# Softmax weights of twelve heads turned by VectorE's blocks and a trip through DRAM instead of by TensorE

## The chip, the core and the metric

The kernel runs on one core of one Trainium2 chip. The core has five engines that run side by side, each through its own queue in order: TensorE (PE in the profile; PEld are its weight loads) multiplies matrices and turns tiles, VectorE (DVE) and ScalarE (ACT) work on elements, GpSimd (POOL) does small elementwise work and can issue transfers, SyncE (SP) issues transfers. Engines wait for one another by semaphores. The metric is the time of one execution in microseconds (us) on the device; the kernel before was run three times.

## The reference

Two layers of an encoder over 256 tokens with 2048 channels, float32. Each layer has a mixer with two kinds of attention, eight heads each, and a gated feed-forward part. Cut to the attention:

```python
def window_attention(q, k, v, sink):          # mixer A, 8 heads, 2 groups of k and v
    s = jnp.einsum('bnqgrd,bnkgd->bgrnqk', qb, kw) * (HEAD_DIM ** -0.5)
    s = jnp.where(mask, s, NEG_INF)
    m = jnp.maximum(jnp.max(s, axis=-1, keepdims=True), snk)
    p = jnp.exp(s - m)
    p = p / (jnp.sum(p, axis=-1, keepdims=True) + jnp.exp(snk - m))
    o = jnp.einsum('bgrnqk,bnkgd->bnqgrd', p, vw)

def neighbourhood_attention(q, k, v, bias_tab):   # mixer B, 8 heads
    s = jnp.einsum('brqhd,brikhd->bhrqik', qg, kg) * (HEAD_DIM ** -0.5)
    s = jnp.where(col_mask, s + bias, NEG_INF)
    p = jax.nn.softmax(s, axis=-1)
    o = jnp.einsum('bhrqik,brikhd->brqhd', p, vg)
```

The softmax weights p of a head are a 256 x 256 matrix. They are made with the query on the partitions, and the product with v needs them with the key on the partitions, so each head's p has to be turned.

## The kernel before, in words

All weights stream once from DRAM in units of 16 blocks of 128x128 (1 MB). `unit_steps` issues the load of a unit on SP's queue (line 286) into one of four buffers; ScalarE makes the high half of each half unit (the cast of line 297) and VectorE the low half (the subtraction of line 298), into one of four half-unit buffers `hl`; TensorE then makes three passes (high x high, high x low, low x high) per block, in `feature_block` (lines 314 to 316, results with features on the partitions) or in `Stream.tokens` (lines 377 to 379, results with tokens on the partitions). So a unit passes through SP, the DMA engines, ScalarE, VectorE and TensorE in this order, and on each engine the work of other units and of the attention stands between.

Work beside the stream is put in by `Paced`: at the end of each unit `tick` first runs what was deferred to it and then moves each background job on by its rate. One job is the list of adaLN columns (line 225 loads 1 MB on SP's queue into the same four buffers, line 226 multiplies and sums it on VectorE). The other is `attention`: one step of it moves each live head to its next `yield` and starts a new head if its q and k are there. In the second layer its rate is `ATT[1]`, 0.4 steps a unit, and from the projection of mixer A on `ATT_B[1]`, 0.21.

A head begins with the splits of its q and k (`in_halves`), then runs `attend`: the scores `sc` (line 607) on TensorE, mask or bias with the maximum on VectorE (line 610), the exponential and the scaling by 1/sum on ScalarE (lines 618 and 626), which leave p of 128 x 2 x 256 in SBUF. At the next step TensorE turns p in four pieces of 128x128 into PSUM (`tp`, line 631), ScalarE and VectorE split it into `pT` (lines 389 and 390, 128x512 each). At the step after that TensorE multiplies it with v (`po`, line 639) and the result is split into `oA` or `oB` (lines 641 and 642). Mixer B's heads load their bias into p first (line 825, on SP's queue). p has two buffers, pT one.

Between, groups of q and k are normalised by `qk_rows`: the sums of squares on ScalarE (line 547), the inverse root on GpSimd (line 441), which is nearly all that GpSimd does, and the multiplication on VectorE (line 556). Their turned rows lie in `packs`: `qTa` holds the eight q of mixer A, each 128x256; in mixer B's pack `b`, the rows `b[:, 8 + i]` hold q and `b[:, i]` hold k of head i. In the second layer q and k are copied into split halves (`SCORES_3`) before the scores, after which those rows are no longer read.

The order of instructions on each engine is set by the scheduler of the framework from the program's order and its own estimates; the order of the changed kernel's instructions is known from its build.

Of the kernel before, what the change touches and what calls it, by code (L numbers as in the profile page):

```python
# [9 lines left out]
F32 = mybir.dt.float32  # L10
F32R = mybir.dt.float32r
# [4 lines left out]
P = 128  # L16
L = 2
D = 2048
S = 256
# [8 lines left out]
NEG = -1e30  # L28
SCALE = HEAD ** -0.5
GRID_W, NA_KH, NA_KW = 64, 8, 16  # L30


QKV_GROUPS = [1024, 0, 512, 2560, 3584, 1536, 3072, 4096, 2048]
# [44 lines left out]

H_RATE = [2.7, 1.7]

ATT = [1.288, 0.4]
ATT_B = [0.21, 0.21]

SCORES_3 = (1,)

ADA_ORDER = [[p * KC + k for k in range(KC) for p in ps] for ps in ((0, 1), (2,), (3, 4), (5,))]
ADA_ORDER = [i for part in ADA_ORDER for i in part]
# [47 lines left out]
def encoder(ctx: ExitStack, tc: tile.TileContext, a: dict, out: bass.AP):  # L135
    nc = tc.nc
    pool = lambda name, bufs, **kw: ctx.enter_context(tc.tile_pool(name=name, bufs=bufs, **kw))
# [12 lines left out]
    ev = pool("ev", 3)  # L150
    at = pool("at", 2)
    sm = pool("sm", 3)
    mm = pool("mm", 4, space=bass.MemoryType.PSUM)
    ax = pool("ax", 3, space=bass.MemoryType.PSUM)

    ident = const.tile([P, P], F32, name="ident")
    make_identity(nc, ident[:])
# [25 lines left out]
    def place(tag, n, dt, name):  # L183
        return sp.tile([P, n, S], dt, name=name, tag=tag)
# [16 lines left out]
    def paired(dt, name):  # L201

        t = ev.tile([P, 2 * S + ROW], dt, name=name, tag="u", bufs=2)
        return t[:, ROW - OFF : ROW - OFF + 2 * S].rearrange("p (a s) -> p a s", a=2)
# [71 lines left out]
                pass  # L276

    bg = Paced()

    def unit_steps(l, u, by_halves=False):  # L280

        raw = rawp.tile([P, UB * P], F32, name=f"w{l}_{u}", tag="raw")
        if not by_halves:
            nc.sync.dma_start(raw[:], a["ws"][l, u])
        halves = []
        streamed = any(m == "w_in" and mo < GATE_A // P for m, _, mo in STREAMS[l][u * UB : (u + 1) * UB])
        at = OFF if streamed else 0
        for j in range(2):  # L290
            n = UB * P // 2
            hl = hlp.tile([P, 2 * n + ROW], F32R, name=f"hl{l}_{u}_{j}", tag="hl")
            hl = hl[:, at : at + 2 * n].rearrange("p (a n) -> p a n", a=2)
            r = raw[:, j * n : (j + 1) * n]
            if by_halves:
                nc.sync.dma_start(r, a["ws"][l, u][:, j * n : (j + 1) * n])
            nc.scalar.copy(hl[:, 0], r)  # L297
            nc.vector.tensor_tensor(out=hl[:, 1], in0=r, in1=hl[:, 0].bitcast(F32), op=ALU.subtract)  # L298
            halves.append(hl)
            if j == 0:  # L300
                yield halves
# [84 lines left out]
    def split(dst, src, scale=None):  # L386

        if scale is None:
            nc.scalar.copy(dst[:, 0], src)
            nc.vector.tensor_tensor(out=dst[:, 1], in0=src, in1=dst[:, 0].bitcast(F32), op=ALU.subtract)  # L390
            return
        nc.scalar.activation(out=dst[:, 0], in_=src, func=AF.Copy, scale=scale)
        nc.vector.scalar_tensor_tensor(
            out=dst[:, 1], in0=src, scalar=scale, in1=dst[:, 0].bitcast(F32), op0=ALU.mult, op1=ALU.subtract
        )
# [202 lines left out]
    def by(x):  # L598

        return ((0, 0), (0, 1), (1, 0))[: 2 * len(x) - 1]  # L600

    def attend(q, k, v, p, mask, scale, sink, o):

        sc = ax.tile([P, 2, S], F32, name="sc", tag="ax")
        for t in range(2):
            for i, j in by(q):
                nc.tensor.matmul(sc[:, t], q[i][:, t * P : (t + 1) * P], k[j], start=i + j == 0, stop=(i, j) == by(q)[-1])  # L607
        m = sm.tile([P, 2], F32, name="m", tag="m")
        for t in range(2):
            nc.vector.tensor_tensor_reduce(  # L610
                out=p[:, t], in0=sc[:, t], in1=mask[:, t], scale=scale, scalar=-3.0e38 if sink is None else sink,
                op0=ALU.add, op1=ALU.max, accum_out=m[:, t : t + 1],
            )
        nm = sm.tile([P, 2], F32, name="nm", tag="nm")
        nc.vector.tensor_scalar(out=nm[:], in0=m[:], scalar1=-1.0, scalar2=None, op0=ALU.mult)
        den = sm.tile([P, 2], F32, name="den", tag="den")
        for t in range(2):
            nc.scalar.activation(out=p[:, t], in_=p[:, t], func=AF.Exp, bias=nm[:, t : t + 1], accum_out=den[:, t : t + 1])
        if sink is not None:
            es = sm.tile([P, 2], F32, name="es", tag="es")  # L620
            nc.scalar.activation(out=es[:], in_=nm[:], func=AF.Exp, bias=sink)
            nc.vector.tensor_tensor(out=den[:], in0=den[:], in1=es[:], op=ALU.add)
        ri = sm.tile([P, 2], F32, name="ri", tag="ri")
        nc.vector.reciprocal(out=ri[:], in_=den[:])
        for t in range(2):
            nc.scalar.activation(out=p[:, t], in_=p[:, t], func=AF.Copy, scale=ri[:, t : t + 1])
        yield
        tp = ax.tile([P, 2, S], F32, name="tp", tag="ax")
        for k in range(2):
            for t in range(2):  # L630
                nc.tensor.transpose(tp[:, k, t * P : (t + 1) * P], p[:, t, k * P : (k + 1) * P], ident[:])  # L631
        pT = at.tile([P, 2, 2, S], F32R, name="pT", tag="pT", bufs=1)
        split(pT, tp[:])
        v = v()
        yield
        po = ax.tile([P, 512], F32, name="po", tag="ax")
        for i, j in by(v):
            for b in range(2):
                nc.tensor.matmul(po[:, :S], v[i][:, b], pT[:, j, b], start=i + j + b == 0, stop=i + b == 2)  # L639
        o = o()  # L640
        nc.scalar.copy(o[:, 0], po[:, :S])
        nc.vector.tensor_tensor(out=o[:, 1], in0=po[:, :S], in1=o[:, 0].bitcast(F32), op=ALU.subtract)
# [91 lines left out]
    tables = []  # L734
# [23 lines left out]
    for l in range(L):  # L758
# [35 lines left out]
        kTa, qTa = packs[0][:, 0:3:2], packs[0][:, 4:12]  # L794
# [3 lines left out]
        oA, oB = [], []  # L798

        def head_a(i):  # L800
            g = i // (HA // GA)
            if i >= 6:
                oA.append(paired(F32R, f"oA{l}_{i}"))
            elif i % 2 == 0:
                o = place(("y0", "y1", "y2")[i // 2], 4, F32R, f"oA{l}_{i}")
                oA.extend((o[:, :2], o[:, 2:]))
            q = in_halves(qTa[:, i], f"qA{l}_{i}", "qh", l in SCORES_3)
            if i % (HA // GA) == 0:
                kvs[0] = in_halves(kTa[:, g], f"kA{l}_{g}", "kh", l in SCORES_3)
            k = kvs[0]  # L810
            yield
            p = at.tile([P, 2, S], F32, name="p", tag="p")

            def v():
                if i % (HA // GA) == 0:
                    kvs[1] = in_halves(packs[0][:, 1:4:2, g * HEAD : (g + 1) * HEAD], f"vA{l}_{g}", "vh", True)
                return kvs[1]

            yield from attend(q, k, v, p, tables[0], SCALE, sink[:, i : i + 1], lambda: oA[i])

        def head_b(hb):
            b, i = packs[1 + hb // 4], hb % 4
            v = b[:, 4:8].rearrange("p (t a) s -> p t (a s)", t=2)
            p = at.tile([P, 2, S], F32, name="p", tag="p")
            nc.sync.dma_start(p[:], a["bias"][l, hb])
            q = in_halves(b[:, 8 + i], f"qB{l}_{hb}", "qh", l in SCORES_3)
            k = in_halves(b[:, i], f"kB{l}_{hb}", "kh", l in SCORES_3)
            yield
            yield from attend(
                q, k, lambda: in_halves(v[:, :, i * HEAD : (i + 1) * HEAD], f"vB{l}_{hb}", "vh", True), p, p, 1.0, None,  # L830
                lambda: oB_of(hb),
            )

        def oB_of(hb):
            if hb == 0:
                o = place("a", 12, F32R, f"oB{l}_{hb}")
                oB.extend(o[:, 2 * i : 2 * i + 2] for i in range(6))
            elif hb == 6:
                oB.extend(chunks_of(sp, "b0", 6, f"oB{l}_{hb}", 2))
            return oB[hb]  # L840
# [30 lines left out]
        for pi, (groups, gates) in enumerate(parts):  # L871
            last = pi == len(parts) - 1
            for g, part in enumerate(groups):
                have_h(part)
                pss = st.tokens(h, part)
                if pi == max(0, len(parts) - 2) and g == 0:
                    gains, sink, cw, rots = small(l)
                dst = packs[g // 3][:, 4 * (g % 3) : 4 * (g % 3) + 4]
                rows = dst.rearrange("p (t a) s -> p t (a s)", t=2)
# [25 lines left out]
                if g == 2:  # L905
                    bg.add(job, ATT[l])

# [26 lines left out]
        if l:  # L934
            bg.pace(job, ATT_B[l])
        gb = []
        for tag in ("y0", "y1", "y2"):
            t = place(tag, 4, F32, f"gb{l}_{tag}")
            gb += [t[:, i] for i in range(4)]
        for i in range(2):  # L940
            t = paired(F32, f"gb{l}_{i}")
# [56 lines left out]
        for gi, chunks in enumerate(FF_GROUPS):  # L998
# [34 lines left out]
            for cs in sets:  # L1033
                fns = [lambda p, e=e, c=c: e(p, c) for c in cs for e in (g_evac, v_evac)]
                src = bare.chunks if gi == 0 and cs[0] < BARE[1] // 2 else bare.h
# [113 lines left out]
```

## Time and profile before

| | us |
|---|---|
| median of 3 runs | 2667.84 |
| lowest and highest run | 2664.56, 2676.24 |
| span of the profiled execution | 2663.2 |
| first layer, first and last of TensorE's turns of p, from the span's start | 281.1, 443.7 |
| second layer, the same | 1518.7, 1796.0 |

The span is that of the profiled execution, from the first to the last instruction. The profile lists for each group of instructions its line, engine, operation, what it writes and reads, shapes, count, busy time and the mean length of one. A timeline gives the start and the length of single instructions and, in brackets, how long the engine was idle before and who released it. The chain of waits goes back from the last instruction to what released each step, so what stands on it sets the time. SPq are SP's issues of transfers.

### The profile page before, as it was taken

To read this page: it belongs to the slowest core of one execution; us is meant where nothing else is said; L and a number is where in the kernel's file an instruction comes from. 1 tells how busy PE (TensorE), PEld (TensorE's weight loads), DVE (VectorE), ACT (ScalarE), POOL (GpSimd) and SP (SyncE) were. 2 spreads that over 40 slices of the span, in tenths; PEclk is the share of its full clock that TensorE was granted. 3 is DMA by queue.
4 is the path that set the end of the run, shared out by engine and by line. 5 is a ranking of instruction groups with operands and counts; after the bars stand their busy time and mean duration, and the time that the engine had idled before them with its cause. 6 is when DMAs were issued, how large, how long until landed. Compare 5 with 4: busy or idle time off the path is not lost.

```text
span 2663.2 us, 50845 instructions
## 1 busy us (share of the span) xinstructions
PE 2650.9 (100%) x21256; PEld 2565.7 (96%) x21256; DVE 2102.2 (79%) x2959; ACT 1412.8 (53%) x2284; POOL 36.2 (1%) x25
## 2 busy tenths in 40 slices
PE   9999999999999999999999999999999999999999
PEld 7888899999999999999998889999999999999999
DVE  8898998997987888788976667768888866655664
ACT  5445865456644555355555566554565445544553
POOL 0001100000000000000000000000000000000000
PEclk9999999999999999999999999999999999999999
DMA  9987789885787878788766666666747765555554
GB/s 372 351 327 292 262 300 352 317 320 199 291 294 287 302 288 295 289 294 289 290 217 254 228 229 231 245 252 253 285 173 288 297 256 190 190 194 194 197 191 143
DMA packets 102039, 700.41 MB, mean 263 GB/s; under 512 B 12721, under 2 KB 15025, under 8 KB 17969
## 3 DMA queue, kind: packets, MB, share of 16 engines
q1 hardware_dynamic: 101810, 697.17, 71.4%
q8 instruction: 166, 2.72, 0.4%
q14 instruction: 63, 0.52, 0.1%
HBM read 695.03 MB, written 2.10 MB: 262 GB/s over the span
## 4 chain that ended last, share of the span: by engine, by line
PE 89%; DVE 6%; ACT 1%; issue 1%; DMA 1%; POOL 0%; SPq 0%; DVEq 0%; ACTq 0%
PE ps L314 25%; PE ps L316 25%; PE ps L315 25%; PE ps_t L377 4%; PE ps_t L379 4%; PE ps_t L378 4%; DVE hl L298 2%; DVE aw L226 2%; DMA aw<-in_aw 1%; PE sc L607 1%; PE po L639 1%; ACT hl L297 1%; PE tp L631 1%; POOL qrs L441 0%; PE qtp L580 0%
## 5 line engine op out<-in xcount | busy, mean ns | idle before, releaser
L298 DVE TENSOR_TENSOR hl<-w,hl 128x1024 fp32r<-128x1024 f32 x928 | 1128.3, 1222 | 360.0 <-ACT hl L297 357.6
L297 ACT CAST hl<-w 128x1024 fp32r<-128x1024 f32 x928 | 970.7, 1049 | 748.5 <-PE ps L316 518.1
L314 PE MATMUL ps<-h,hl 128*128 128x256 f32 x3328 | 922.8, 277 | 1.3 <-DVE ya L915 0.6
L315 PE MATMUL ps<-h,hl 128*128 128x256 f32 x3328 | 919.8, 276 | 0.0
L316 PE MATMUL ps<-h,hl 128*128 128x256 f32 x3328 | 919.8, 277 | 0.0
L314 PEld LDWEIGHTS ps<-h,hl 128*128 128x128 f32 x3328 | 624.8, 188 | 2.4 <-DVE ya L915 0.8
L315 PEld LDWEIGHTS ps<-h,hl 128*128 128x128 f32 x3328 | 625.3, 188 | 0.4 <-DVE h L470 0.2
L316 PEld LDWEIGHTS ps<-h,hl 128*128 128x128 f32 x3328 | 624.4, 188 | 0.0
L226 DVE CUSTOM_DVE_ANT_0 aw<-aw,cact,ab 128x2048 f32<-128x2048 f32 x189 | 443.5, 2347 | 48.8 <-DMA aw<-in_aw 47.8
L377 PE MATMUL ps_t<-hl,h 128*128 128x512 f32 x576 | 223.1, 392 | 2.6 <-ACT h L469 2.1
L378 PE MATMUL ps_t<-hl,h 128*128 128x512 f32 x576 | 224.9, 391 | 0.3
L379 PE MATMUL ps_t<-hl,h 128*128 128x512 f32 x576 | 224.3, 390 | 0.0
L994 DVE SCALAR_TENSOR_TENSOR u<-ps,cw,u 128x255 f32<-128x255 f32 x304 | 146.1, 481 | 66.5 <-ACT u L992 62.2
L992 ACT ACTIVATE u<-ps,cw 128x256 f32<-128x256 f32 x152 | 85.9, 565 | 187.9 <-PE ps L316 187.5
L316 PE MATMUL ps<-merged,hl 128*128 128x256 f32 x512 | 141.8, 277 | 0.4 <-DVE hl L298 0.4
L315 PE MATMUL ps<-merged,hl 128*128 128x256 f32 x512 | 141.6, 277 | 0.0
L314 PE MATMUL ps<-merged,hl 128*128 128x256 f32 x512 | 141.6, 277 | 0.0
L315 PE MATMUL ps<-act_o,hl 128*128 128x256 f32 x512 | 141.4, 276 | 0.0
L316 PE MATMUL ps<-act_o,hl 128*128 128x256 f32 x512 | 141.3, 276 | 0.0
L314 PE MATMUL ps<-act_o,hl 128*128 128x256 f32 x512 | 141.2, 276 | 0.0
L377 PEld LDWEIGHTS ps_t<-hl,h 128*128 128x128 f32 x576 | 107.9, 188 | 26.1 <-ACT h L469 3.1
L378 PEld LDWEIGHTS ps_t<-hl,h 128*128 128x128 f32 x576 | 108.1, 188 | 23.7 <-DVE hl L298 1.9
(231 smaller groups left out, 4612.5 us busy)
## 6 DMA issues: line engine op xcount, KB each, us to landing
w<-in_ws SPq DMA_DIRECT2D x463, 1024.0 KB, 4.9
aw<-in_aw SPq DMA_DIRECT2D x189, 1024.0 KB, 6.1
p<-in_bias SPq DMA_DIRECT2D x16, 256.0 KB, 4.2
x<-in_xT SPq DMA_DIRECT2D x4, 512.0 KB, 5.3
aw_o<-in_aw SPq DMA_DIRECT2D x2, 1024.0 KB, 12.3
out<-x SPq DMA_DIRECT2D x16, 128.0 KB, 2.1
w<-in_ws SPq DMA_DIRECT2D x2, 512.0 KB, 11.7
aw_b<-in_aw SPq DMA_DIRECT2D x1, 1024.0 KB, 18.1
```

The source lines that it names most:

```text
L226: nc.vector.tensor_tensor_reduce(out=raw[:], in0=raw[:], in1=cact[:], scale=1.0, scalar=ab[:, i : i + 1], op0=ALU.mult, op1=ALU.add, accum ...
L297: nc.scalar.copy(hl[:, 0], r)
L298: nc.vector.tensor_tensor(out=hl[:, 1], in0=r, in1=hl[:, 0].bitcast(F32), op=ALU.subtract)
L314: nc.tensor.matmul(out, hi, act[0], start=first, stop=False)
L315: nc.tensor.matmul(ps[:, :S], hi, act[1], start=False, stop=False)
L316: nc.tensor.matmul(out, lo, act[0], start=False, stop=last)
L377: nc.tensor.matmul(ps[:], xh, hi, start=kc == kcs[0], stop=False)
L378: nc.tensor.matmul(ps[:], xh, lo, start=False, stop=False)
L379: nc.tensor.matmul(ps[:], xl, hi, start=False, stop=kc == kcs[-1])
L607: nc.tensor.matmul(sc[:, t], q[i][:, t * P : (t + 1) * P], k[j], start=i + j == 0, stop=(i, j) == by(q)[-1])
L992: nc.scalar.activation(out=u, in_=ps, func=AF.Identity, scale=w[:, 1:2], bias=w[:, 3:4])
L994: nc.vector.scalar_tensor_tensor(out=u[:, to], in0=ps[:, of], scalar=w[:, j : j + 1], in1=u[:, to], op0=ALU.mult, op1=ALU.add)
```

## The change

Twelve heads of the second layer, the first six of each mixer (`MOVED`), no longer turn p on TensorE. `attend` takes `rows`, two stretches of 128x256 that nothing reads any more: for mixer A the head's own q in `qTa` and a spare tile (tag "r", two buffers), for mixer B the head's own q and k in `b`. VectorE's `transpose` turns p in blocks of 32x32 into these rows, one instruction for each half of the queries. GpSimd's queue then writes them to a DRAM tile `pY` (two buffers): for each half and each 32 partitions one transfer, eight in a head, each of 32 KB in 256 pieces of 128 bytes that bring every block to its place. Three units later (`BACK`, by way of `later`), or when the head needs it, SP's queue brings the two halves back into the same rows, 128 KB each; SP waits there for all eight writes. Two steps more than before lie between, then ScalarE and VectorE split the rows into `pT`, two pieces of 128x256 each. The rates become `ATT[1]` 0.42 and `ATT_B[1]` 0.32. The other four heads of the second layer and all of the first stay as they were.

```diff
+BLOCK = 32
...
-ATT = [1.288, 0.4]
-ATT_B = [0.21, 0.21]
+ATT = [1.288, 0.42]
+ATT_B = [0.21, 0.32]
...
+BACK = 3
+MOVED = [(0, 0), (6, 6)]
...
+    dram = pool("dram", 2, space=bass.MemoryType.DRAM)
...
+    def once(fn):
+        due = [fn]
+        def run():
+            if due:
+                due.pop()()
+        return run
+
+    def later(n, fn):
+        if n == 0:
+            fn()
+        else:
+            bg.defer(lambda: later(n - 1, fn))
+
+    def turned_blocks(p, rows):
+        y = dram.tile([P, 2, S], F32, name="pY", tag="pY")
+        to = y[:].rearrange("(b i) k (t a j) -> t a i k b j", i=BLOCK, t=2, a=P // BLOCK)
+        for t, row in enumerate(rows):
+            nc.vector.transpose(out=row, in_=p[:, t])
+            src = row.rearrange("p (k b j) -> p k b j", k=2, j=BLOCK)
+            for a in range(P // BLOCK):
+                nc.gpsimd.dma_start(to[t, a], src[a * BLOCK : (a + 1) * BLOCK])
+        return y
...
-    def attend(q, k, v, p, mask, scale, sink, o):
+    def attend(q, k, v, p, mask, scale, sink, o, rows=None):
...
+        if rows is not None:
+            rows = rows()
+            y = turned_blocks(p, rows)
+            def back():
+                for k in range(2):
+                    nc.sync.dma_start(rows[k], y[:, k])
+            back = once(back)
+            later(BACK, back)
+            yield
+            yield
+            back()
+            pT = at.tile([P, 2, 2, S], F32R, name="pT", tag="pT", bufs=1)
+            for k in range(2):
+                split(pT[:, :, k], rows[k])
+        else:
             tp = ax.tile([P, 2, S], F32, name="tp", tag="ax")
...
+            def rows():
+                spare = ev.tile([P, S], F32, name=f"spare{l}_{i}", tag="r", bufs=2)
+                return [qTa[:, i], spare[:]]
...
+                q, k, v, p, tables[0], SCALE, sink[:, i : i + 1], lambda: oA[i], rows if i < MOVED[l][0] else None
...
+                lambda: oB_of(hb), (lambda: [b[:, 8 + i], b[:, i]]) if hb < MOVED[l][1] else None,
```

More of the change, by code (lines that the diff above doesn't have):

```diff
@@ L627, in attend @@
         yield
[L628 to L633, printed above, removed]
+        if rows is not None:
[13 more added lines that the diff above has]
+        else:
+            tp = ax.tile([P, 2, S], F32, name="tp", tag="ax")
+            for k in range(2):
+                for t in range(2):
+                    nc.tensor.transpose(tp[:, k, t * P : (t + 1) * P], p[:, t, k * P : (k + 1) * P], ident[:])
+            pT = at.tile([P, 2, 2, S], F32R, name="pT", tag="pT", bufs=1)
+            split(pT, tp[:])
         v = v()
@@ L817, in v @@
                 return kvs[1]
-            yield from attend(q, k, v, p, tables[0], SCALE, sink[:, i : i + 1], lambda: oA[i])
+            def rows():
+                spare = ev.tile([P, S], F32, name=f"spare{l}_{i}", tag="r", bufs=2)
+                return [qTa[:, i], spare[:]]
+            yield from attend(
+                q, k, v, p, tables[0], SCALE, sink[:, i : i + 1], lambda: oA[i], rows if i < MOVED[l][0] else None
+            )
         def head_b(hb):
@@ L830, in head_b @@
                 q, k, lambda: in_halves(v[:, :, i * HEAD : (i + 1) * HEAD], f"vB{l}_{hb}", "vh", True), p, p, 1.0, None,
-                lambda: oB_of(hb),
+                lambda: oB_of(hb), (lambda: [b[:, 8 + i], b[:, i]]) if hb < MOVED[l][1] else None,
             )
```

## The prediction

> **What bounds the kernel now.** I read the page first, then the chain of waits and the stretch of the second layer's attention (1505 to 1800 us). The page:
>
> ```profile
> span 2663.2 us, 50845 instructions
> PE 2650.9 (100%) x21256; PEld 2565.7 (96%) x21256; DVE 2102.2 (79%) x2959; ACT 1412.8 (53%) x2284; POOL 36.2 (1%) x25
> ...
> PE 89%; DVE 6%; ACT 1%; issue 1%; DMA 1%; POOL 0%; SPq 0%; DVEq 0%; ACTq 0%
> ...
> out<-x SPq DMA_DIRECT2D x16, 128.0 KB, 2.1
> ```
>
> TensorE (PE) is busy for the whole span and carries 89% of the chain, so what leaves TensorE leaves the time, and what makes it wait is added. The span is 4.6 us below the runs' median of 2667.84 us; I make the sum against the span and add it to the median. In the stretch itself (one row of the busy time by windows; columns: PE, PEld, DVE, ACT, POOL busy, clock, DMA share, GB/s):
>
> ```profile
> 1505.00:1800.00 295.00, 294.94 (x2194) 278.97 (x2193) 204.38 (x331) 175.18 (x350) 4.91 (x3) 1.00 0.64 236
> ```
>
> TensorE never waits, VectorE is 69% busy, ScalarE 59%, the DMA engines 64%, GpSimd idle. Nothing is short; only lateness can hurt.
>
> **What is removed.** Four transposes per head leave TensorE. The chain of waits shows what they take there:
>
> ```profile
> 1518.85 0.44 PE tp L631 x4
> 1519.28 0.71 PE sc L607 x6
> 1536.41 0.71 PE po L639 x6
> 1537.12 0.44 PE tp L631 x4
> 1537.55 0.70 PE sc L607 x6
> 1549.16 0.71 PE po L639 x6
> ```
>
> 12 heads x 0.44 us = **-5.3 us**, the whole gain. In the built order 16 of the layer's 64 transposes stay (four heads), so the change does what it says. The new paces 0.42 and 0.32 move no TensorE work in or out.
>
> **What VectorE and ScalarE get.** Per head the copy and the split of 128x512 become two of 128x256 each, and VectorE gets two turns of 128x256, an operation that the trace does not show.
>
> ```profile
> L389 ACT CAST pT<-tp x16: 577/595/619, 1519.8 to 1796.7; 128x512 fp32r<-128x512 f32 x16
> L390 DVE TENSOR_TENSOR pT<-tp,pT x16: 679/681/691, 1521.1 to 1798.0; 128x512 fp32r<-128x512 f32 x16
> ...
> 1511.10 0.42 DVE L390 TENSOR_TENSOR qA<-packA,qA 128x256 fp32r<-128x256 f32 x1
> ```
>
> With 0.42 us for each 128x256 piece, VectorE gets 4 x 0.42 - 0.68 = 1.0 us a head, 12 us in all; bounds for a turn are 0 and 1.2 us (the 128x1024 subtractions below). VectorE's 90 idle us in the stretch cover it, except where the splitting of a weight stands right behind; the cover being in pieces, I take a third, **+4** (0 to 12).
>
> **What GpSimd gets: the price that decides.** 96 transfers of 32 KB, eight a head, each of 256 pieces of 128 bytes. The trace has no transfer by GpSimd. Nearest rows (the tile p in this stretch, the timeline of GpSimd, and the groups of the whole span, busy time and mean ns):
>
> ```profile
> L825 SPq DMA_DIRECT2D p<-in_bias x8: 327/328/423, 1617.9 to 1738.1; - x8
> ...
> DMA to landing us min/median/max: 2.6/3.4/5.1
> ...
> 1534.64 1.64 POOL L441 TENSOR_TENSOR qrs<-qss,mhalf 128x8 f32<-128x8 f32 x1 [42.82 <-DVE qss L440]
> 1562.91 1.64 POOL L441 TENSOR_TENSOR qrs<-qss,mhalf 128x8 f32<-128x8 f32 x1 [26.63 <-DVE qss L440]
> ...
> L441 POOL TENSOR_TENSOR qrs<-qss,mhalf 128x8 f32<-128x8 f32 x12 | 27.8, 2320 | 258.3 <-DVE qss L440 258.3
> ```
>
> From below 0.33 us (SP's issue), from above 2.32 us (GpSimd's mean over its twelve 128x8 operations). I take **1.64 us**, GpSimd's own row in this stretch: the same engine, in the same surroundings, and 256 pieces are more work than SP's issue of 128 rows. So 13.1 us a head. The write's landing I take from the 128 KB stores, 2.1 us, the return's (2 x 128 KB) between that and the 3.4 us of a 256 KB load, 2.7 us.
>
> [...]
>
> **First head of mixer A.** Its turns stand on VectorE between the two subtractions of 1515.33 and 1517.24, its copy back on ScalarE between the casts of 1526.31 and 1528.22 (timelines of the three engines; start, length, engine, line):
>
> ```profile
> 1515.21 0.90 ACT L626 ACTIVATE p<-p,ri 128x256 f32<-128x256 f32 x2
> ...
> 1526.31 1.03 ACT L297 CAST hl<-w 128x1024 fp32r<-128x1024 f32 x1
> 1528.22 1.05 ACT L297 CAST hl<-w 128x1024 fp32r<-128x1024 f32 x1 [0.87 <-PE ps_t L379]
> ...
> 1515.33 1.23 DVE L298 TENSOR_TENSOR hl<-w,hl 128x1024 fp32r<-128x1024 f32 x1 [0.58 <-ACT hl L297]
> 1517.24 1.23 DVE L298 TENSOR_TENSOR hl<-w,hl 128x1024 fp32r<-128x1024 f32 x1 [0.68 <-ACT hl L297]
> ...
> 1538.09 0.40 PE L377 MATMUL ps_t<-hl,h 128*128 128x512 f32 x1
> ```
>
> First turn done at 1517.0, eight writes at 1530.1, landed 1532.2, returned about 1535.2. ScalarE wants it at 1527.3 and stands 8 us, with the cast of the next weight behind it. That weight is first used at 1538.09 (unit 33) and needs 1.05 + 1.23 us before: cover 7.6 us. Nearly all is hidden; what queues up behind costs **+2** (0 to 8).
>
> **The norm behind the writes.** GpSimd's 1.64 us operation of 1534.64 (rsqrt of a q group) now stands behind 17 writes: eight from 1517.0 and eight more end at 1543.2, the third head's first write at 1544.9 (its turn and the DRAM buffer, of which there are two, are there by then), the operation at 1546.5. VectorE waits for it, with a weight's subtraction behind:
>
> ```profile
> 1536.31 1.29 DVE L556 TENSOR_TENSOR qn<-ps_t,qrs 128x512 f32<-128x512 f32 x2 [1.81 <-POOL qrs L441]
> 1537.52 2.35 DVE L298 TENSOR_TENSOR hl<-w,hl 128x1024 fp32r<-128x1024 f32 x2
> ...
> 1543.56 0.39 PE L377 MATMUL ps_t<-hl,h 128*128 128x512 f32 x1
> ```
>
> That second subtraction then ends at 1546.5 + 1.3 + 1.2 = 1549.0. It belongs to the second half of unit 34, which TensorE begins at 1543.56 and reaches 2.7 us later, 1546.3: **+3** (0 to 17, at 2.32 us a write).
>
> **First head of mixer B** has its turns at about 1632 (beside the subtraction of 1632.61) and its copy ahead of the cast of 1642.74, again some 10 us for 13.1 + 2.1 + 2.7:
>
> ```profile
> 1632.61 1.23 DVE L298 TENSOR_TENSOR hl<-w,hl 128x1024 fp32r<-128x1024 f32 x1 [1.76 <-ACT hl L297]
> ...
> 1642.74 1.05 ACT L297 CAST hl<-w 128x1024 fp32r<-128x1024 f32 x1 [1.42 <-PE ps L316]
> ...
> 1652.55 0.28 PE L314 MATMUL ps<-h,hl 128*128 128x256 f32 x1
> ```
>
> Late 8 us, cover 1652.55 - 1642.74 - 2.3 = 7.5 us, scores and po queued behind: **+4** (0 to 12).
>
> **The other ten heads** have 25 us or more to their copy, but each return stands in SP's queue ahead of a weight, and SP waits there for all eight writes. How much SP can lose:
>
> ```profile
> 1528.35 5.29 SPq L286 DMA_DIRECT2D w<-in_ws  x3
> 1539.90 0.33 SPq L225 DMA_DIRECT2D aw<-in_aw  x1
> ...
> w<-in_ws SPq DMA_DIRECT2D x51, 1024.0 KB, 5.2
> ...
> 1541.04 1.05 ACT L297 CAST hl<-w 128x1024 fp32r<-128x1024 f32 x1 [2.34 <-PE ps_t L379]
> ```
>
> The weight issued at 1528.35 lands 5.2 us later and is cast at 1541.04: 7.5 us to spare, plus some 7 us between cast and use, so about 14. The heads' scores above come at 1519.28, 1537.55 and 1550.31, 15.5 us apart at the pace of 0.4; at 0.42 that is 14.8 us, at mixer B's 0.32 19 us. GpSimd's 13.1 us fits, but half a head's lateness is passed on. The second head's return waits until 1545.3 for a weight issued at about 1533.3: 12 us, just inside. At that nearness I take 1.2 us a head, **+12** (0 to 40). The 24 issues on SP (0.33 us each) fall into its waits. The DMA engines get 6.3 MB more, out and back, beside 72.65 MB in 310 us:
>
> ```profile
> q1 hardware_dynamic: 10852, 72.65, 63.8%
> ```
>
> By bytes that is 6.3 / 72.65 x 63.8 = 5.5% of their time, of 36% free: nothing. If a piece of 128 bytes took as long as a packet does now (0.638 x 16 x 310 / 10852 = 0.29 us), 24,576 of them would take 446 us on each of 16 engines and could not fit; I stay near the bytes, because a 128 KB store in pieces of 1 KB, eight to an engine, lands in 2.1 us with all its latency.
>
> **Sum:** -5.3 + 4 + 2 + 3 + 4 + 12 = **+19.7 us**. The profiled execution's span of 2663.2 us becomes 2682.9; with the 4.6 us to the median that is **about 2688 us**, slower by 0.7%.
>
> **Rivals.** *Hidden.* A write costs GpSimd 1.0 us or less. Then the 17 writes and the norm end by 1542, where VectorE, later in its new order, asks for it anyway; ScalarE's wait of 3 us lies inside its cover; SP waits under 6 us. What is left is -5.3 and +4, with 0 to 8 for the edges: 2662 to 2675, 2667 in the middle, not slower than can be told. For it: SP's 0.33 us and the idle GpSimd. Against: 256 pieces a transfer. It decides below 1.2 us a write.
>
> *GpSimd-bound.* From 1.85 us a write (14.8 / 8) GpSimd falls behind in mixer A. At 2.32 us: six heads x (18.6 - 14.8) = 23, the norm 17, mixer B's first head 6, the rest of B 12, VectorE 4, less 5.3: +57, 2725 us. For it: the 2.32 us mean. Against: 1.64 us in this very stretch.
>
> *GpSimd held by VectorE.* If it could write only while VectorE is idle (31%), 96 x 1.64 = 157 us would take 510 us of a 295-us stretch: +200, 2870 us. Against: the three operations by GpSimd here all took 1.64 us beside a busy VectorE. [...]
>
> **How the numbers follow.** Forecast 0.43, hidden 0.33, GpSimd-bound 0.17, held 0.04; 0.03 for a gain that I see no source for. The measurement tells 0.5% (13 us) from no change. Same: nine tenths of hidden and a sixth of the forecast's own range (2676 to 2705), 0.37; slower 0.60; faster 0.03, since 5.3 us is all there is to win. The range, 2660 to 2760, leaves out the lock, the far end of GpSimd-bound and the unexplained gain. Hidden's share lies on the other side, so the forecast's own range stands beside it: 2676 to 2705.
>
> **What would show it.** GpSimd's transfers: mean length, and whether eight take 13 us. SP's wait ahead of a return; ScalarE's pT copy in mixer A's first head waiting 8 us for a DMA; VectorE's qn waiting 5 us or more for qrs; TensorE idle some 25 us between 1520 and 1740, nothing elsewhere. Wrong if a write takes under 1.2 or over 1.85 us, if the pieces of 128 bytes slow the weights' landing past 5.2 us, or if TensorE waits where none of these stands.

## The result, and the profile after

| | before | after |
|---|---|---|
| median of 8 runs, us | 2671.86 | 2685.62 |
| lowest and highest, us | 2664.56, 2676.24 | 2678.79, 2694.91 |
| ratio, 95% interval | | 1.0055 (1.0037 to 1.0072) |
| profiled execution: span (time), us | 2663.2 | 2690.0 (2691.89) |

The change makes the kernel 13.8 us slower by the medians. The forecast was 2688. The page of the kernel after (parts 3, 4 and 6):

```profile
q0 software_dynamic: 3072, 3.15, 0.5%
PE 60%; DMA 19%; DVE 11%; issue 7%; ACT 2%; POOL 1%; SPq 0%; DVEq 0%; POOLq 0%; ACTq 0%
pY<-packB POOLq DMA_DIRECT2D x48, 32.0 KB, 3.6
packB<-pY SPq DMA_DIRECT2D x12, 128.0 KB, 2.3
```

and the transfers from 1490 to 1830:

```profile
w<-in_ws SPq DMA_DIRECT2D x52, 1024.0 KB, 6.0
```

TensorE is still the busiest engine (99%), but the chain now runs through transfers for 19% of the span (1% before), nearly all of it adaLN columns that VectorE waits for at line 231. Most of this is not the change's doing. From 500 to 1490 us both kernels run the same instructions, and VectorE waits there 93.8 us for columns (26.9 before); `paces` below, which has no trip and is no slower, waits 85.3 and has 12% transfers on its chain, and `back_later`, the order of the change once more, has 4%. What the change adds lies behind: 38.6 us from 1490 to 1970, 7.7 before. Over the whole span the weights land as before (5.0 us, 4.9 before), but from 1490 to 1830 they take 6.0 us, 5.3 before.

**Where the extra time lies.** GpSimd's last inverse root ahead of the moved heads (`qrs`) and its next one behind the attention (`nrs`) stand in both kernels, so their distance is the time of the changed stretch. The timeline of GpSimd, before:

```profile
1490.18 1.64 POOL L441 TENSOR_TENSOR qrs<-qss,mhalf 128x8 f32<-128x8 f32 x1 [21.30 <-DVE qss L440]
1938.96 0.70 POOL L457 TENSOR_TENSOR nrs<-nss,mhalf 128x2 f32<-128x2 f32 x1 [323.97 <-DVE nss L519]
```

and after:

```profile
1500.89 1.64 POOL L474 TENSOR_TENSOR qrs<-qss,mhalf 128x8 f32<-128x8 f32 x1 [21.30 <-DVE qss L473]
1965.73 0.71 POOL L490 TENSOR_TENSOR nrs<-nss,mhalf 128x2 f32<-128x2 f32 x1 [213.07 <-DVE nss L552]
```

448.78 us have become 464.84, 16.1 more. The other 10.7 us between the two spans lie ahead of 1500, where both kernels run the same instructions. This execution was one of the longer ones (2691.89 against a median of 2685.62), and a later run with the same order of instructions (`back_later` below) has 15.3 us in the stretch and none ahead of it. The stretch is therefore what I compare from here on, beside the medians. It is read from one execution of each run; the only repetition, 15.3 against 16.1, differs by 0.8 us.

**What TensorE lost there.** Busy time by windows, after (columns: PE, PEld, DVE, ACT, POOL busy, granted clock, DMA share, GB/s):

```profile
1505.00:1800.00 295.00, 282.89 (x1957) 261.21 (x1956) 203.22 (x355) 166.00 (x346) 63.98 (x99) 0.98 0.68 244
...
1580.00:1600.00 20.00, 16.74 (x76) 13.28 (x75) 13.63 (x24) 10.42 (x21) 5.48 (x9) 0.91 0.65 226
...
1640.00:1660.00 20.00, 17.21 (x134) 16.82 (x133) 13.26 (x23) 10.68 (x22) 3.70 (x6) 0.91 0.70 230
...
1700.00:1720.00 20.00, 16.31 (x117) 15.84 (x116) 9.54 (x21) 6.06 (x13) 3.47 (x6) 0.83 0.79 295
```

TensorE is idle for 12.1 us of the 295 (0.06 before), and 9.7 of them lie in the three windows shown, 3.3, 2.8 and 3.7 us; each holds one long stop, of 3.0, 2.8 and 3.4 us. In the same windows the granted clock falls to 0.91, 0.91 and 0.83, which is another (0.09 + 0.09 + 0.17) x 20 = 7.0 us. Idle time and clock make 19.1 us; less the 5 us of transposes that are gone, 14 of the 16.1. The clock in single matmuls, timeline of TensorE around the second stop:

```profile
1647.63 0.74 PE L689 MATMUL po<-pT,vA 128*128 128x256 f32 x4 [2.78 <-DVE pT L423]
...
1650.10 0.41 PE L349 MATMUL ps<-h,hl 128*128 128x256 f32 x1
```

After 2.8 us without work a matmul takes 0.41 us instead of 0.28, until 1652. In windows cut to the slow matmuls behind the three stops (1590.44 to 1593.85, 1648.47 to 1651.88, 1713.32 to 1720.15) the granted clock is 0.50. The three stops cost 7.0 us of clock to their 9.7 us of idle time, some 70% more than their length. But not every such stop costs clock. In `back_later`, the same order of instructions, one of 3.0 us has none:

```profile
1570.00:1590.00 20.00, 16.67 (x83) 13.43 (x82) 12.57 (x23) 11.49 (x21) 4.93 (x8) 1.00 0.67 236
1577.53 0.50 PE L411 MATMUL ps_t<-hl,h 128*128 128x512 f32 x1 [3.01 <-DVE hl L331]
```

**What GpSimd does.** Its transfers by the tile pY, with what its queue idled for, after:

```profile
L310 POOL DMA_DIRECT2D pY<-packB x48: 612/612/656, 1655.0 to 1752.0; - x48
...
issue: 63.2, 35
```

and the first head's eight in its timeline:

```profile
1527.96 2.00 POOL L310 DMA_DIRECT2D pY<-packA  x3 [25.43 <-DVE spare L307]
1534.80 0.62 POOL L310 DMA_DIRECT2D pY<-packA  x1 [4.84 <-issue]
1535.41 1.22 POOL L310 DMA_DIRECT2D pY<-spare  x2
1538.49 1.23 POOL L310 DMA_DIRECT2D pY<-spare  x2 [1.86 <-issue]
```

A transfer holds GpSimd for 0.61 us, far under the 1.64 that I took. But after three of them it stands still for 4.8 us, and no semaphore that the profile shows releases it ("issue"). Its end goes with the landings: the first three writes land at 1534.5 to 1534.8, 5.5 to 6.5 us after their issue, and the fourth goes out at 1534.80. Of the 93 writes behind the first three none begins before the write three ahead of it has landed, and 34 of the 35 pauses end 0.25 to 0.38 us after that landing. The first head's eight, 4.9 us of work, take from 1527.96 to 1539.72, 11.8 us. Over the twelve heads they take 8.7 to 18.9 us, half of them under 11.2.

**Who waits.** Waits of SP's transfer queue from 1490 to 1860, after:

```profile
SPq L667 <- DMA pY<-spare: 44.5, 18, 7.0
SPq L667 <- DMA pY<-packB: 41.9, 17, 7.1
```

and of the engines from 1490 to 1830, after (us in total, times, longest):

```profile
DVE aw L231 <- DMA aw<-in_aw: 37.8, 11, 10.5
DVE qn L589 <- POOL qrs L474: 8.4, 4, 2.5
ACT pT L422 <- DMA packA<-pY: 6.5, 1, 6.5
ACT pT L422 <- DMA packB<-pY: 4.2, 1, 4.2
```

SP stands 86 us ahead of the returns, waiting for the writes. What it would have issued next comes late, and VectorE, which takes its work in order, waits 38 us for adaLN columns (7.4 before). The third stop of TensorE shows the chain; timelines of SP, VectorE and TensorE, after:

```profile
1699.63 0.80 SPq L667 DMA_DIRECT2D packB<-pY  x2
1700.54 0.37 SPq L319 DMA_DIRECT2D w<-in_ws  x1
1701.02 0.36 SPq L230 DMA_DIRECT2D aw<-in_aw  x1
...
1711.07 2.35 DVE L231 CUSTOM_DVE_ANT_0 aw<-aw,cact,ab 128x2048 f32<-128x2048 f32 x1 [10.46 <-DMA aw<-in_aw]
...
1713.91 0.56 PE L347 MATMUL ps<-oA,hl 128*128 128x256 f32 x1 [3.42 <-DVE ya L436]
```

The return goes out at 1699.63, a weight and the columns right behind it, bunched; the columns land 9.9 us later, VectorE has been idle for 10.5 us, and TensorE waits for what VectorE does after them.

The first stop goes back to GpSimd. From the chain of waits between 1505 and 1830, after (start, length, what):

```profile
1549.86 2.53 issue
...
1553.03 1.68 POOL qrs L474
...
1555.34 1.23 DVE hl L331
1556.58 6.67 DMA aw<-in_aw
...
1578.88 1.68 POOL qrs L474
...
1594.21 7.04 DMA aw<-in_aw
...
1615.58 7.50 DMA aw<-in_aw
...
1701.02 9.91 DMA aw<-in_aw
```

From 1527.96 on the chain runs through the writes of the first heads and their pauses to the norm of 1553.03, which stands behind them on GpSimd. VectorE's subtraction of a weight comes behind that norm, and with its end the columns of 1556.58 go out, which VectorE waits for next. The lateness goes on from there to the norm of 1578.88 and to the subtraction for which TensorE stops 3.0 us, until 1589.09. The write just ahead of that later norm adds little: its input was there at 1578.05, so the norm is 0.8 us late, and in `writes_only` below no write holds it and the stop (2.3 us) comes all the same. Three of the four landings of columns shown, 7.0, 7.5 and 9.9 us, were issued behind a return and a weight, within 1.5 us of the return. Ahead of the second stop VectorE waited 1.6 us for columns and then worked without a gap up to the split that TensorE needed.

### The profile page after: what moved, and what is told of

It reads as the page before. It is cut to its first block, busy times and chain, and to the rows that moved or that the text cites. A ratio compares the mean times of both kernels' runs of the same rounds, so it can differ in the third digit from the quotient of the medians.

```text
span 2690.0 us, 51046 instructions
## 1 busy us (share of the span) xinstructions
PE 2659.7 (99%) x21208; PEld 2568.4 (95%) x21208; DVE 2106.1 (78%) x2995; ACT 1400.6 (52%) x2296; POOL 94.9 (4%) x121
## 3 DMA queue, kind: packets, MB, share of 16 engines
q0 software_dynamic: 3072, 3.15, 0.5%
## 4 chain that ended last, share of the span: by engine, by line
PE 60%; DMA 19%; DVE 11%; issue 7%; ACT 2%; POOL 1%; SPq 0%; DVEq 0%; POOLq 0%; ACTq 0%
DMA aw<-in_aw 17%; PE ps L347 17%; PE ps L349 17%; PE ps L348 16%; DVE hl L331 5%; PE ps_t L412 3%; PE ps_t L410 3%; PE ps_t L411 3%; DVE aw L231 3%; ACT hl L330 1%; DVE u L1050 1%; POOL pY L310 1%; DMA w<-in_ws 1%; PE sc L640 1%; PE po L689 1%
## 5 line engine op out<-in xcount | busy, mean ns | idle before, releaser
L1048 ACT ACTIVATE u<-ps,cw 128x256 f32<-128x256 f32 x152 | 85.3, 561 | 128.0 <-PE ps L349 127.9
```

The source lines that it names most:

```text
L1048: nc.scalar.activation(out=u, in_=ps, func=AF.Identity, scale=w[:, 1:2], bias=w[:, 3:4])
```

## The experiments

The table gives for each run its median, the ratio to before with its 95% interval, and the stretch from `qrs` to `nrs` against the 448.8 us of before. The medians of before in the three groups of runs were 2668.18, 2669.21 and 2664.56.

| run | median | ratio (95%) | stretch, us against before |
|---|---|---|---|
| the change | 2685.62 | 1.0055 (1.0037 to 1.0072) | +16.1 |
| no_trip | 2660.43 | 0.9974 (0.9963 to 0.9984) | -5.0 |
| ring_short | 2788.45 | 1.0447 (1.0426 to 1.0468) | +122.0 |
| ring_same | 2703.87 | 1.0136 (1.0119 to 1.0152) | +14.2 |
| ring_long | 2692.89 | 1.0099 (1.0084 to 1.0114) | +5.6 |
| pool_back | 2683.56 | 1.0059 (1.0040 to 1.0077) | +9.6 |
| paces | 2668.50 | 1.0002 (0.9991 to 1.0013) | -1.2 |
| pieces_back | 2671.90 | 1.0013 (1.0001 to 1.0025) | +4.1 |
| a_only | 2677.97 | 1.0036 (1.0023 to 1.0050) | +9.5 |
| writes_only | 2664.41 | 0.9997 (0.9988 to 1.0006) | -0.1 |
| back_later | 2680.22 | 1.0057 (1.0045 to 1.0070) | +15.3 |
| pieces_later | 2665.35 | 1.0001 (0.9991 to 1.0010) | -2.1 |
| act_writes | 2684.89 | 1.0076 (1.0063 to 1.0088) | +20.7 |

**Without the trip: `no_trip`.**

```diff
-            for a in range(P // BLOCK):
-                nc.gpsimd.dma_start(to[t, a], src[a * BLOCK : (a + 1) * BLOCK])
...
-                    nc.sync.dma_start(rows[k], y[:, k])
```

> Left out: all transfers of the trip to DRAM and back; VectorE still turns the blocks of the twelve heads, and the products use the rows as they are (32x32 blocks turned, but not put in their places). Theory 1 (the trip costs, through GpSimd's pauses and SP's waits at the returns): with no transfer nothing waits, and what is left is -5.3 us on TensorE and at most +4 us on VectorE and ScalarE: 0.5 to 6 us below the time before, VectorE's waits for aw back under 10 us in the stretch. Rival (the extra operations of VectorE and ScalarE, or the new paces, cost): the time stays 8 us or more above the time before.

5.0 us less in the stretch, as expected; 7.8 by the medians, above the 6 expected, but with an interval of 4.3 to 9.9. Waits of VectorE from 1490 to 1860:

```profile
DVE aw L230 <- DMA aw<-in_aw: 7.3, 7, 2.4
```

As before the change. So the turns on VectorE, the finer splits and the new paces cost nothing that can be told, the gain of 5 us is real, and the trip alone costs 16.1 + 5.0 = 21.1 us of the stretch.

**The writes without the returns: `writes_only`.**

```diff
-                for k in range(2):
-                    nc.sync.dma_start(rows[k], y[:, k])
```

> The eight writes of each head stay, the two returns are left out (the products use the turned rows where they are, so the blocks are not put in their places). Theory 1 (SP's waits at the returns delay the weights): without them aw's wait is under 12 us and the time 2660 to 2668, at most 7 above the run without the trip. Rival (GpSimd's paused writes themselves, ahead of the norms and beside the weights): 2672 or more, with VectorE's wait for qrs still 8 us and TensorE's gap for the weight behind it still there.

Waits of the engines from 1490 to 1860:

```profile
DVE qn L589 <- POOL qrs L474: 11.9, 4, 6.4
DVE aw L231 <- DMA aw<-in_aw: 9.3, 7, 3.4
PEld ps_t L411 <- DVE hl L331: 3.8, 2, 2.7
```

GpSimd pauses as long as in the change (65 us), the norms are late, and TensorE still waits for the weight behind a norm; but the adaLN columns are on time again. One wait for a norm is 6.4 us long, and the chain leads from that norm, the one of 1553.03 in the change, to the only long stop of TensorE (2.3 us, with a granted clock of 0.93 in its 20 us). The writes thus cost 5 us (-0.1 against -5.0), through the norms, and the returns the other 16.1 (+16.1 against -0.1). Theory 1 fits three quarters of the loss, the rival the rest. What this run can't tell apart is how the returns cost: without them SP's waits are gone, but also ScalarE's for returned rows (10.7 us) and the traffic.

**The scratch size: `ring_short`, `ring_same`, `ring_long`.**

```diff
-    nc = _bacc.Bacc("TRN2", target_bir_lowering=False, num_devices=1, dynamic_dma_scratch_size=1024)
+    nc = _bacc.Bacc("TRN2", target_bir_lowering=False, num_devices=1, dynamic_dma_scratch_size=512)
```

In the expectations I call what this size sets GpSimd's descriptor space; what it holds, no run shows.

> GpSimd's descriptor space is cut from 1024 to 512 bytes, so that one transfer fits at a time instead of three. Theory 1 (GpSimd's 0.61 us transfers pause because the space is full until earlier ones have landed): it pauses after every transfer for some 3 us, eight take 25 to 35 us instead of 9 to 13, more than the 15 to 19 us between heads; the time rises by 40 to 150 us over the changed kernel's. [...]

With 1536 bytes go three other edits; the control has them too, with 1024 bytes:

```diff
-    skip(96, const)
-    skip(224)
...
-                sq = at.tile([P, HEAD], F32, name="qsq", tag="qsq", bufs=1)
+                sq = at.tile([P, HEAD], mybir.dt.bfloat16, name="qsq", tag="qsq", bufs=1)
```

> Control for the next: the space stays 1024 bytes, but the scratch tile of the squares is bfloat16 (its content is never read) and two unused tiles are gone, which moves the addresses of all others. Both theories: within 5 us of the changed kernel's 2685.6, pauses as there.

> The same as the control with 1536 bytes of descriptor space, room for five transfers instead of three. Theory 1: the first pause comes after five transfers, eight take 6 to 10 us, pauses in the stretch fall from 63 to under 35 us, VectorE's wait for aw falls from 38 to under 25 us, the time is 3 to 10 us below the control's. Rival (what delays the weights is the traffic of 128-byte pieces or SP's wait for the landing, which a longer ring does not change): within 3 us of the control's.

Waits of GpSimd from 1490 to 1860 with 512 bytes (`ring_short`),

```profile
POOL pY L310 <- issue: 203.8, 83, 6.4
```

its timeline in the first head,

```profile
1521.25 0.79 POOL L310 DMA_DIRECT2D pY<-packA  x1 [25.43 <-DVE spare L307]
1525.92 0.63 POOL L310 DMA_DIRECT2D pY<-packA  x1 [3.89 <-issue]
```

the waits with 1536 bytes (`ring_long`),

```profile
POOL pY L308 <- issue: 13.0, 11, 3.2
```

and the timeline there:

```profile
1529.16 2.61 POOL L308 DMA_DIRECT2D pY<-packA  x4 [25.45 <-DVE spare L305]
1531.76 0.61 POOL L308 DMA_DIRECT2D pY<-spare  x1
1534.26 1.83 POOL L308 DMA_DIRECT2D pY<-spare  x3 [1.89 <-issue]
```

One, three or five transfers go out before the first pause with a size of 512, 1024 or 1536 bytes. The first head's eight take 21.0 (a little less than the 25 to 35 expected), 11.8 and 6.9 us, the pauses 204, 63 and 13 us. The time follows: 103 us above the change by the medians with the short one (106 in the stretch); with the long one 11 us below its control by the medians and 8.6 in the stretch, and VectorE's wait for the columns falls from 36.6 to 23.1 us. So GpSimd's pauses go by this size, and with 1024 bytes they end as earlier writes land (34 of 35, above). That the space is full while it pauses fits both, but no profile shows the space itself.

The control missed its expectation: 2703.87 instead of 2685.6 give or take 5. Its stretch is that of the change (+14.2), so what the moved addresses or the other tile cost, some 18 us by the medians, lies outside it; in the profiled executions 11.7 us lie ahead of the stretch and 10.4 behind. Which of the three edits does it was not tried, and the pair is read only against each other.

**The return on GpSimd's queue: `pool_back`.**

```diff
-                    nc.sync.dma_start(rows[k], y[:, k])
+                    nc.gpsimd.dma_start(rows[k], y[:, k])
```

> The two returns of each head are issued by GpSimd's queue instead of SP's, so that GpSimd waits for its eight writes to land and SP goes on to the next weight. Theory 1 (SP's wait at the returns delays weights and aw, and TensorE with them): VectorE's wait for aw in the stretch falls from 38 to under 15 us and the time from 2685.6 to 2664 to 2676. Rival (what costs is GpSimd's own lateness, for the norms and the casts of pT): aw's wait falls too, but VectorE's wait for qrs rises from 8 to over 15 us and ScalarE's for the returned rows over 11 us; the time stays at 2680 or more.

Waits of GpSimd from 1490 to 1860:

```profile
POOL packA L667 <- DMA pY<-spare: 19.7, 5, 5.3
POOL packB L667 <- DMA pY<-packB: 17.7, 5, 5.4
```

The wait for the columns falls from 37.8 to 15.7 us, just missing its mark of 15, and the time does not follow: 2683.6, as the rival had it, though the wait for the norms rose only to 10.9, not over 15. GpSimd now waits for its own writes (37 us) with the next head's writes queued behind. The two measures differ here: by the medians moving the wait to another queue moved the loss with it, by the stretch of one execution (+9.6 against +16.1) 6.5 us of the loss went. So this run doesn't settle theory 1.

**The new paces alone: `paces`.**

```diff
-ATT = [1.288, 0.4]
-ATT_B = [0.21, 0.21]
+ATT = [1.288, 0.42]
+ATT_B = [0.21, 0.32]
```

> The kernel before with the new paces of the second layer's heads alone (0.42 and 0.32 for 0.4 and 0.21), nothing turned, no trip. Theory 1 (the paces move no work in or out): within 3 us of before. Rival (the paces alone bring part of what the run without the trip gained beyond 5.3 us): 2 to 5 us below before; or they cost: 4 us or more above.

No difference, as theory 1 had it.

**Mixer A alone: `a_only`.**

```diff
-MOVED = [(0, 0), (6, 6)]
+MOVED = [(0, 0), (6, 0)]
```

> Only mixer A's first six heads go by the trip, the new paces stay. By the two traces the changed kernel was 9 us behind where mixer B's heads begin and 16 at the end, the run without the trip 5 us ahead at both. Theory 1 (the trip costs in both mixers, by lateness that adds up): 5 to 11 us above before. Rival (mixer A's heads hide their trip, and mixer B's six make the loss): within 4 us of before; or mixer A makes all of it: 12 us or more.

8.8 us above before by the medians, 9.5 in the stretch: both mixers cost, mixer A's six heads somewhat more than half.

**The pieces on the way back: `pieces_back`.**

```diff
-            for a in range(P // BLOCK):
-                nc.gpsimd.dma_start(to[t, a], src[a * BLOCK : (a + 1) * BLOCK])
+            nc.gpsimd.dma_start(y[:, t], row)
...
-                    nc.sync.dma_start(rows[k], y[:, k])
+                    for b in range(P // BLOCK):
+                        nc.sync.dma_start(
+                            rows[k][b * BLOCK : (b + 1) * BLOCK].rearrange("i (t a j) -> i t a j", t=2, j=BLOCK),
+                            y[:].rearrange("(a i) t (k b j) -> k b i t a j", i=BLOCK, k=2, j=BLOCK)[k, b],
+                        )
```

> The blocks are put in their places on the way back: GpSimd writes each half of a head in one transfer of 128 rows of 1 KB (two a head instead of eight), and SP fetches each row half in four transfers of 256 pieces of 128 bytes (eight a head instead of two). The result is the reference's. Theory 1 (GpSimd's pauses for a full descriptor space are most of the cost): its pauses fall from 63 to under 10 us, SP's issues grow by 72 x 0.35 = 25 us that its waits absorb, and the time is 2664 to 2677. Rival (the 128-byte pieces cost on the DMA engines, whoever sends them): 2680 or more, weights landing in over 6 us.

The transfers by the tile pY:

```profile
L665 SPq DMA_DIRECT2D packB<-pY x48: 557/611/2733, 1641.7 to 1728.0; - x48
...
L307 POOL DMA_DIRECT2D pY<-packB x12: 539/539/578, 1635.5 to 1717.0; - x12
...
issue: 0.4, 1
```

The pauses are gone, and the same computation takes 2671.9, 0.13% above before: theory 1 by its time. The sign of the rival came too: from 1490 to 1830 the weights land in 6.7 us (5.3 before, 6.0 in the change), and ScalarE waits 31.5 us for them there (1.9 in the change). The rival's time did not, so the weights land later where SP sends the pieces, which costs little. SP's waits at the returns are no measure of the loss either: they fell only from 86 to 73 us, while VectorE's wait for columns fell from 37.8 to 11.2. An issue of 256 pieces takes SP 0.61 us, not the 0.35 that I wrote.

**One step later: `back_later` and `pieces_later`.**

```diff
-BACK = 3
+BACK = 4
```

> The changed kernel with the return due one step of a weight's half later (BACK 4 for 3, some 6 us). Theory 1: SP's waits at the returns fall from 86 to under 45 us and the time by 4 to 12 us, to 2674 to 2682. Rival (GpSimd's pauses cost by the norms and pT): within 4 us of 2685.6, aw's wait still over 30 us.

The scheduler put every instruction of the changed kernel where it had stood, on each engine, so this run tests neither theory. It is a second measurement of the change: 1.0057 against 1.0055, SP's waits 86.7 us.

> The run with the pieces on the way back, with the return one step later too. Theory 1 (what that run still loses, 2671.9 against 2660.4 without the trip, is SP's 73 us of waits at the returns): SP's waits fall to under 40 us and the time to 2661 to 2668, below before. Rival (SP's eight issues a head, some 0.7 us each, and the traffic are what is left): within 3 us of 2671.9.

Here the returns did move behind weights. SP's waits at them fell from 72.6 to 51.4 us (not under 40), the stretch from +4.1 to -2.1, and the ratio from 1.0013 to 1.0001. The two intervals overlap. The weights land as late as in `pieces_back` (6.5 us), and VectorE's wait for columns is 6.5 us, as before the change. That is the fastest version with the trip that was run; it equals the kernel before and does not beat it.

**The writes by ScalarE's queue: `act_writes`.**

```diff
-                nc.gpsimd.dma_start(to[t, a], src[a * BLOCK : (a + 1) * BLOCK])
+                nc.scalar.dma_start(to[t, a], src[a * BLOCK : (a + 1) * BLOCK])
```

> The eight writes of each head are issued by ScalarE's queue instead of GpSimd's; the returns stay with SP. Theory 1 (GpSimd's descriptor space is what makes the pauses): another queue has no pause after three, eight writes take under 5 us, and SP's waits at the returns fall to under 50 us; ScalarE pays 96 issues of 0.35 to 0.7 us, 34 to 67 us, which its idle third takes in part: 2668 to 2682. Rival (any queue that sends 256 pieces of 128 bytes stalls behind the weights): ScalarE stalls as GpSimd did, with the casts of the weights behind it: 2700 or more.

ScalarE's timeline in the first head:

```profile
1516.11 2.91 ACTq L310 DMA_DIRECT2D pY<-packA  x4
1519.12 4.47 ACTq L310 DMA_DIRECT2D pY<-spare  x4
```

There is no standstill after three; eight go out in 7.5 us here and in 5.5 to 12.3 over the heads. But ScalarE's own next work, with the casts of the weights, stands behind them, and the time is 2684.9, between the two forecasts (2668 to 2682 and 2700 or more). SP still waits 60 us at the returns, over the 50 that theory 1 allowed. The standstill after three came on GpSimd's queue and not on ScalarE's; there the writes cost ScalarE 34.8 us of idle time ahead of its exponentials (line 651, five waits).

## Why the prediction came out right, and where its steps did not

**The gain of 5.3 us:** 5.0 in `no_trip`. Right.

**VectorE and ScalarE, +4:** mis-sized. A turn takes 0.44 us, close to the 0.42 taken, but the idle pieces of VectorE cover all of it; `no_trip` leaves no more than a few tenths.

**GpSimd, 1.64 us a transfer and 13.1 a head:** this step failed. A transfer takes 0.61 us. By its own words the prediction was wrong if a write took under 1.2 us, and the hidden rival's condition was met, yet that rival's time of 2667 did not come. Eight transfers take 8.7 to 18.9 us all the same, because GpSimd pauses, 63 us in all, while three writes have not landed; with the other two sizes the first pause comes after one and after five. The forecast's time survived because 11 us, the middle of what eight take, is near the 13.1 that I had from a wrong price. That is luck. The forecast and its rivals were all put in the time of one transfer, and none asked how many may be under way. The landing of a write, 2.1 us in my sums, was mis-sized too: 3.0 to 4.5 us, the medians of the three source tiles. Of that, GpSimd is held for 0.61 us; the rest up to the landing holds it only where three writes are under way.

**First head of mixer A, +2, and of mixer B, +4:** ScalarE waited 6.5 and 4.2 us for the returned rows where I had 8 each (a return lands in 2.3 us, 2.7 taken). Neither shows as a stop right behind it: TensorE is idle for 0.85 us from 1520 to 1560 and for 0.06 from 1660 to 1680, so +2 and +4 were too much there. What lateness they hand on is in the sums below.

**The norm, +3:** the place was right. The norm that I named came 7.7 us later than before, counted from `qrs`, behind 17 writes, and it stands on the chain to the first stop (3.0 us, with 1.8 of clock). VectorE's wait for the norms in all hardly grew (8.4 us, 7.3 before): the sign I gave, one wait of 5 us, did not come in the change, where VectorE was itself late from ScalarE's wait for the returned rows. It came in `writes_only` (6.4 us), which puts the cost at 5 us with everything else that the writes do. The upper end of my range was 17 us for this; the sum gives 15.

**The other ten heads, +12:** the place was right. SP waits 86 us ahead of the returns, and the returns cost 16.1 us of the stretch with the first heads' waits in it, where I had 2 + 4 + 12 = 18. The carrier was not: I measured the slack of the weights, 14 us, and not that of the adaLN columns in the same queue, which VectorE waits for in order. Over the runs with the writes on GpSimd's queue the loss goes more with VectorE's wait for columns (7.3 us in `no_trip`, 11.2 in `pieces_back`, 37.8 in the change) than with SP's waits.

**The DMA engines, nothing:** right for the writes, open for the returns. I called myself wrong if the pieces slowed the weights past 5.2 us; in the same window, 1490 to 1800, they land in 6.0. The pieces from GpSimd are not the reason: `writes_only` sends them all, and the weights land in 5.0 us there. Left are the returns and the bunching behind them, which no run separates.

**The whole, +19.7:** by the medians 13.8 us were measured, by the stretch 16.1. That 2688 lies so near 2686 owes something to the kernel before, whose median was 2667.84 us in the three runs I started from and 2671.86 in all eight.

**TensorE idle some 25 us between 1520 and 1740:** 12.1, and 7.0 more that my sum had no term for, the lower clock after the stops.

Of the rivals, the GpSimd-bound case is what `ring_short` made: eight take 20 us and more against 15 to 19 between heads, and the loss is 120 us. Held by VectorE was not seen: a transfer by GpSimd takes 0.61 us at the least and 0.78 at the most, and 34 of the 35 pauses end with the landing of a write.

What stays open: how the cost of the returns divides between SP's waits, the late rows and the traffic, the 10.7 us ahead of the stretch in the one profiled execution of the change, and the 18 us that the control of `ring_long` costs.

## What to carry to other kernels

Price a transfer by GpSimd in three numbers, not one: how long it holds the engine (0.61 us here), how long it takes to land (3.0 to 4.5 us), and how many may be under way before the engine stands still (three here; with the other sizes the first pause came after one and after five); two transfers a head of 128 rows instead of eight of 256 pieces took the pauses from 63 us to 0.4, and the loss in the stretch from 16.1 us to 4.1. When a queue gets a new wait, take the slack of everything behind it, the work that is not the main stream too: SP's 86 us ahead of the returns went on as a wait of VectorE for columns, 37.8 us against 7.4, with TensorE behind it. Count a stop of TensorE of some 3 us at up to 1.7 times its length: in the change the three cost 9.7 us of idle time and 7.0 of clock, while in `back_later` two of four had no lower clock behind them. And compare a share of the whole span with a run of the same instructions before laying it to the change: most of VectorE's longer wait for columns lay where nothing had changed (93.8 us against 26.9 from 500 to 1490).

## What the runs showed of the hardware that I had not expected

- The two kinds of transfer by GpSimd hold it nearly equally long: 0.61 us for 32 KB in 256 pieces, 0.54 us for 128 KB in 128 rows (`pieces_back`).
- How many packets the 128-byte pieces make goes by the queue: 12 heads x 2048 pieces went out in 3072 packets from GpSimd (queue q0, 0.5% of the 16 engines' span) and in 26,112 from ScalarE (`act_writes`, queue q10, 0.8%), which is in number one for each piece and 16 for each transfer. Even so they are far cheaper than the 446 us an engine of my upper bound: 0.8% of the span is 21 us.
- The issue of 256 pieces takes SP 0.61 us and ScalarE 0.62, that of a plain 128 KB return 0.33 to 0.40.
- Gaps of 2.8 to 3.4 us on TensorE were followed by a granted clock of 0.50 for 3.4 to 6.8 us, with matmuls of 0.41 us instead of 0.28. In `back_later` two of four stops of 2.2 to 3.0 us were followed by it and two were not.
